# Other wait counts between projections, transposes and attention bursts in a two-layer hybrid decoder kernel

## The chip, the cores and the metric

The kernel runs on one core of a Trainium2 chip. The metric is the device time of one execution in microseconds (us); a kernel's time is the median of its runs. The five engines of a core work side by side, each on its own list of instructions, and meet through semaphores: PE (matmuls and transposes), DVE (vector), ACT (scalar, activation functions), POOL and SP (which here issues the large loads).

## The reference

Two layers, each a token mixer and an FFN, on 256 tokens of width 1024, in 32-bit floats. The attention in the mixer has two head groups of 8 heads each; with 256 tokens the block-sparse group (MoBA) is plain causal attention over one block, and the DSA group keeps, for each query, the 64 keys that a small indexer scores highest.

```python
def token_mixer(h, w_in, g_moba_out, g_dsa_out, w_out, cos, sin):
    proj = h @ w_in
    mq, mk, mv, dq, dk, dv, qi, ki, wi = jnp.split(proj, offs, axis=-1)
    ...
    o_moba = moba_attention(mq, mk, mv)
    o_dsa = dsa_attention(dq, dk, dv, qi, ki, wi)
    o = jnp.concatenate([rms_norm(o_moba, g_moba_out), rms_norm(o_dsa, g_dsa_out)], axis=-1)
    return o @ w_out
...
for l in range(DEPTH):
    mod = c_act @ w_ada[l] + b_ada[l]
    sh_m, sc_m, gt_m, sh_f, sc_f, gt_f = jnp.split(mod[:, None, :], N_MOD, axis=-1)
    h = rms_norm(x, g_pre_mix[l]) * (1.0 + sc_m) + sh_m
    y = token_mixer(h, w_in[l], g_moba_out[l], g_dsa_out[l], w_out[l], cos, sin)
    x = x + gt_m * rms_norm(y, g_post_mix[l])
    h = rms_norm(x, g_pre_ffn[l]) * (1.0 + sc_f) + sh_f
    y = conv_glu_ffn(h, w_up_act[l], w_up_lin[l], w_conv[l], b_conv[l], w_down[l])
    x = x + gt_f * rms_norm(y, g_post_ffn[l])
```

## The kernel before

**Precision by splits.** Every weight comes from DRAM as a raw tile of 128x1024 floats. ACT rounds it to a high half `wh` (L139), DVE subtracts to get the low half `wl` (L140), and a product is three matmuls: high by high, high by low, low by high. There are five buffers for `wh` and five for `wl`, and a projection of 512 columns takes four of each, so only one tile of the next projection can be split ahead.

**Projections.** A mixer projects mq, mk, mv, dq, dk, dv (512 columns each) for two halves t of the tokens. `project` issues, per t, 16 matmuls with `wh` (two between yields) and then 8 with `wl` (three between yields), all at L391. Layer 0's indexer, mq and mk are computed earlier, in the opening stage; its mv comes first in what follows. ACT then scales and evicts a result (L353, or L801 for the values), DVE rotates its first columns (L357, L362).

**What runs beside a projection.** Everything else is a chain of Python generators in `Background`. Each `yield` of the main work is one tick; a chain's `yield n` means that it goes on n ticks later. So a wait of 5 ticks puts a chain's next step some 10 matmuls further down the recorded program. The chains that matter here:

- "T" and "D": `heads_T` waits, then transposes a head group of q or k (4 transposes at L368, a copy at L369). In layer 0 all steps of T (indexer, mq, mk) stand in one chain behind one another; a chain that has not ended is run out by `drain`, with no matmuls of a projection between its steps.
- "att": first the indexer (a burst of matmuls at L411, relus L431 on ACT, weighted sums L434 on DVE), which waits until T is empty; then `attend` for each group. It works in three sets. A set is a burst of scores (L411) into PSUM banks 4 and 5, DVE's maxima (L475) and ACT's exponentials (L479), a scaling by the reciprocal of the sums (L482, then L485 on ACT or L487 on DVE), two `turn`s (4 transposes each, L494, and a copy L496) and, once the next set's scores are issued, a burst of `values` (L411) with its squares (L517, L518 on ACT; L520, L522 on DVE).
- "top0", "top1": `choose` finds the 64 best keys by eight pairs of MAX (L445) and MATCH_REPLACE (L446) on DVE.
- "out": `group_out` normalizes a head group (two short matmuls L549, a power on POOL, a transpose L556, then L560 to L562).
- "sf" and "gt": `gemv_v` on DVE (L189) and `gemv_p` on PE (a burst of 32 matmuls printed at L411, its transposes L210) compute the adaLN modulation from more weights.

**Order.** A scheduler places the recorded instructions on each engine's list; the order of recording is its main input. The loads are different: SP issues them from the stream in the order in which `load` was called, and the DRAM layout follows that order. A load waits until one of six `raw` buffers is free.

Of the kernel before, what the change touches and what calls it, by code (L numbers as in the profile page):

```python
# [17 lines left out]
D = 1024  # L18
# [56 lines left out]
def trunk(ctx: ExitStack, tc, plan, x, c, stream, small, rope, out):  # L75
# [8 lines left out]
    bg = Background()  # L84
# [7 lines left out]
    def tp_bank():  # L92
        tps["n"] += 1
        return bank(tps["free"][tps["n"] % len(tps["free"])])
# [4 lines left out]
    def big(name, dt=F32):  # L99
        return wrk.tile([128, 4, S], dt, name=name, tag="big", bufs=6)  # L100

    def tiny(n):
        return wrk.tile([128, n], F32, name=f"tiny{n}", tag=f"tiny{n}", bufs=8)


    st = {"off": 0, "behind": ()}
# [257 lines left out]
    def heads_T(src, dst, t, wait):  # L364
        yield wait
        p = tp_bank()
        for j in range(4):
            nc.tensor.transpose(p[:, 128 * j:128 * j + 128], src[:, 128 * j:128 * j + 128], ident)  # L368
        nc.scalar.copy(dst[:, :, 128 * t:128 * t + 128], p.rearrange("p (j t) -> p j t", j=4))  # L369
# [83 lines left out]
    def attend(qT, kT, v, masks, k0, oh, ol, ready):  # L453
# [36 lines left out]
        def turn(i, par):  # L490
            e = live[i, par][0]
            tp = tp_bank()
            for j in range(4):
                nc.tensor.transpose(tp[:, 128 * j:128 * j + 128], e[:, 128 * j:128 * j + 128], ident)  # L494
            eT = t2()
            nc.scalar.activation(out=eT, in_=tp, func=AF.Copy)  # L496
            live[i, par][0] = eT

        def values(i):

            t, b = sets[i]
            nb = t + 1
            nh = 4 // nb
            eT = [live.pop((i, par))[0] for par in range(2)]
            if t not in outs:
                outs[t] = [wrk.tile([128, 512], F32, name="o", tag="o", bufs=3), []]
            po = tp_bank()
            vk = [v[:, 2 * k:2 * k + 2, :].rearrange("p a b -> p (a b)") for k in range(nb)]
            head = lambda j, par: 64 * (2 * (b * nh + j) + par)
            burst([(po[64 * par:64 * par + 64, 128 * j:128 * j + 128],  # L510
                    vk[k][:, head(j, par):head(j, par) + 64],
                    eT[par][:, 128 * (j * nb + k):128 * (j * nb + k) + 128],
                    dict(start=k == 0, stop=k == nb - 1))
                   for j in range(nh) for k in range(nb) for par in (1, 0)])
            sq = t2()
            n = 128 * nh
            nc.scalar.activation(out=sq[:, :n], in_=po[:, :n], func=AF.Square)  # L517
            nc.scalar.activation(out=outs[t][0][:, n * b:n * b + n], in_=po[:, :n], func=AF.Copy)  # L518
            if nh == 4:
                nc.vector.tensor_tensor(out=sq[:, :256], in0=sq[:, :256], in1=sq[:, 256:], op=OP.add)  # L520
            ss = wrk.tile([128, 128], F32, name="ss", tag="ss", bufs=2)
            nc.vector.tensor_tensor(out=ss, in0=sq[:, :128], in1=sq[:, 128:256], op=OP.add)  # L522
            outs[t][1].append(ss)
# [3 lines left out]
        for i in range(len(sets)):  # L527
            while masks is not None and sets[i][0] not in masks:
                yield 1
            scores(i)  # L530
            if i:
                while sets[i - 1][0] not in ready:
                    yield 1
                values(i - 1)
                if sets[i - 1][0] != sets[i][0]:
                    bg.add("out", group_out(sets[i - 1][0], *outs[sets[i - 1][0]], k0, oh, ol))
            yield 3
            turn(i, 0)
            yield 1
            turn(i, 1)  # L540
            yield 2
# [3 lines left out]
    def group_out(t, o, ss, k0, hh, hl):  # L545

        p = tp_bank()
        for i, part in enumerate(ss):
            nc.tensor.matmul(p[:, :1], lhsT=part, rhs=mean, start=i == 0, stop=i == len(ss) - 1)  # L549
        s = tiny(1)  # L550
        nc.vector.tensor_scalar(out=s, in0=p[:, :1], scalar1=EPS, scalar2=None, op0=OP.add)
        r = tiny(1)
        nc.gpsimd.tensor_tensor(out=r, in0=s, in1=mhalf, op=OP.pow)
        yield 7
        p = tp_bank()[:, :128]
        nc.tensor.transpose(p, r.to_broadcast([128, 128]), ident)  # L556
        ks = slice(k0, k0 + 4)
        tt = slice(128 * t, 128 * t + 128)
        ov = o.rearrange("p (k t) -> p k t", k=4)
        nc.vector.tensor_tensor(out=ov, in0=ov, in1=p[:, None, :].to_broadcast([128, 4, 128]), op=OP.mult)  # L560
        nc.scalar.activation(out=hh[:, ks, tt], in_=ov, func=AF.Copy)
        nc.vector.tensor_tensor(out=hl[:, ks, tt], in0=ov, in1=hh[:, ks, tt].bitcast(F32), op=OP.subtract)  # L562
        st["out"] += 1
        yield
# [198 lines left out]
    for l in range(DEPTH):  # L763

        qiT = big("qT")
# [3 lines left out]
        def idx_out(b, t, a):  # L769
            if b == 0:  # L770
                qs[t] = t2()
                kis[t] = wrk.tile([128, 128], F32, name="ki", tag="ki", bufs=2)
                wis[t] = wrk.tile([128, 8], F32, name="wi", tag="wi", bufs=2)
            q, ki = qs[t], kis[t]
            rope_out(a[:, :256].rearrange("p (h d) -> p h d", d=HD),
                     q[:, 256 * b:256 * b + 256].rearrange("p (h d) -> p h d", d=HD), t, True, 4)
            if b == 0:
                rope_out(a[:, None, 256:320], ki[:, None, :64], t, False, 1)
                nc.scalar.activation(out=wis[t], in_=a[:, 320:], func=AF.Copy, scale=8.0 ** -0.5)
                nc.vector.tensor_copy(ki[:, 64:], ki[:, :64])  # L780
                return
            bg.add("T", heads_T(q, qiT, t, 5))
            bg.add("T", ki_T(ki, t))

        def ki_T(ki, t):
# [2 lines left out]
            nc.scalar.copy(kiT[:, 128 * t:128 * t + 128], p[:, :128])  # L788
            yield 1

        def qk_done(dst, is_q, chain="T", wait=5):
            def f(t, a):
                r = t2()
                rope_out(a.rearrange("p (h d) -> p h d", d=HD), r.rearrange("p (h d) -> p h d", d=HD), t, is_q, 8)
                bg.add(chain, heads_T(r, dst, t, wait))
            return f
# [8 lines left out]
        def run_project(name, done, first=()):  # L805
            late = "h" if name in ("ia", "ib") else "w" if name != "dv" else None
            bg.run(project(l, name, hh, hl, (0, 1, 2), done, first, late))
# [17 lines left out]
        masks = {}  # L825
# [20 lines left out]
        dqT, dkT, dv = big("qT"), big("kT"), big("v")  # L846
        if l == 0:
            bg.add("sf", gemv_v(l, 32, 40, 9))
        run_project("dq", qk_done(dqT, True, "D", 10))
        run_project("dk", qk_done(dkT, False, "D", 7))  # L850
        bg.add("att", attend(dqT, dkT, dv, masks, 4, oh, ol, ready[1]))
        run_project("dv", v_done(dv, ready[1]))
        bg.drain("T", "D", "ada", "gt")
# [210 lines left out]
```

## Time and profile before

| | |
|---|---|
| median of 3 runs | 690.02 us (689.62 to 690.02) |
| profiled execution | 689.88 us, of it 688.1 us span |
| granted TensorE clock | 0.999 of full speed |
| PE busy | 664.8 us, 97% |
| DVE busy | 547.6 us, 80% |
| ACT busy | 424.8 us, 62% |
| chain that ended last | PE 76%, DVE 12%, ACT 6%, issue 3% |

The span is the stretch from the first to the last instruction of the profiled execution; about 1.8 us lie around it. Busy shares are averages over stages with different limits. The chain that ended last is followed backwards from the last instruction, at each step to what released it. On a timeline a bracket such as [1.09 <-DVE tiny L475] says how long the engine was idle before the instruction, and what ended the wait.

### The profile page before, as it was taken

The numbers are of one execution on the slowest core, as the hardware profiler recorded it, in microseconds if no ns is written. First come the engines' busy times: TensorE is split into PE (matmuls) and PEld (weight loads), VectorE is DVE, ScalarE is ACT, GpSimd is POOL, SyncE is SP. The second block draws the span as 40 slices with busy tenths as digits, with TensorE's granted clock in tenths as the row PEclk, the third lists the DMA queues.
The fourth block names the chain that finished last, engine by engine and source line by source line (L and its number), as shares of the span: only waits on it lengthen the run. The fifth ranks groups of instructions, "written<-read, shape, count | busy, mean of one in ns | idle before, by whom it ended". The sixth has DMA issues, their size and how long they took to land.

```text
span 688.1 us, 11317 instructions
## 1 busy us (share of the span) xinstructions
PE 664.8 (97%) x4329; PEld 569.6 (83%) x4329; DVE 547.6 (80%) x1085; ACT 424.8 (62%) x787; POOL 26.2 (4%) x56
## 2 busy tenths in 40 slices
PE   7999898999999999999999999999999999999996
PEld 4887676777999999999988677777789999999994
DVE  5878999878899999897679985677689886666553
ACT  5556687886955555555576558878696555555441
POOL 1000000002000000000020000000200000000001
PEclk9999999999999999999999999999999999999999
DMA  8999558963499998987436642346246885655001
GB/s 362 419 415 372 181 203 332 370 219 123 183 332 379 379 361 340 340 328 281 168 140 245 275 133 114 123 168 220 103 172 232 320 316 183 217 184 184 1 1 61
DMA packets 24518, 163.04 MB, mean 237 GB/s; under 512 B 3312, under 2 KB 3728, under 8 KB 6160
## 3 DMA queue, kind: packets, MB, share of 16 engines
q1 hardware_dynamic: 23184, 159.77, 61.8%
q0 software_dynamic: 704, 2.11, 1.0%
q8 instruction: 34, 0.56, 0.3%
q10 hardware_dynamic: 576, 0.43, 0.2%
q14 instruction: 20, 0.16, 0.1%
HBM read 161.24 MB, written 1.06 MB: 236 GB/s over the span
## 4 chain that ended last, share of the span: by engine, by line
PE 76%; DVE 12%; ACT 6%; issue 3%; POOL 1%; DMA 1%; SPq 0%; POOLq 0%; DVEq 0%; ACTq 0%
PE b L569 18%; PE b L567 18%; PE b L568 18%; PE b L391 12%; PE b L726 3%; DVE wl L140 3%; PE b L411 2%; DVE iscore L434 2%; ACT t L479 1%; DVE iscore L446 1%; ACT t L254 1%; DVE tiny L445 1%; PE b L494 1%; DVE raw L684 1%; DMA raw<-in_stream_dram 1%
## 5 line engine op out<-in xcount | busy, mean ns | idle before, releaser
L140 DVE TENSOR_TENSOR wl<-raw,wh 128x1024 fp32r<-128x1024 f32 (+1 forms) x146 | 172.8, 1195 | 36.9 <-ACT wh L139 31.3
L567 PE MATMUL b<-hh,wh 128*128 128x256 f32 x640 | 179.9, 281 | 0.0
L569 PE MATMUL b<-hl,wh 128*128 128x256 f32 x640 | 179.6, 281 | 0.0
L568 PE MATMUL b<-hh,wl 128*128 128x256 f32 x640 | 179.6, 281 | 0.0
L139 ACT ACTIVATE wh<-raw 128x1024 fp32r<-128x1024 f32 (+1 forms) x146 | 149.0, 1047 | 41.9 <-PE b L569 37.0
L568 PEld LDWEIGHTS b<-hh,wl 128*128 128x128 f32 x640 | 122.5, 191 | 1.3
L567 PEld LDWEIGHTS b<-hh,wh 128*128 128x128 f32 x640 | 120.2, 188 | 1.5
L569 PEld LDWEIGHTS b<-hl,wh 128*128 128x128 f32 x640 | 120.1, 188 | 0.0
L189 DVE SCALAR_TENSOR_TENSOR raw<-raw,crow 128x1024 f32<-128x1024 f32 x72 | 86.6, 1218 | 1.9 <-DMA raw<-in_stream_dram 1.9
L391 PE MATMUL b<-wh,hh 128*128 128x512 f32 (+1 forms) x184 | 73.0, 399 | 0.1
L391 PE MATMUL b<-wh,hl 128*128 128x512 f32 (+1 forms) x184 | 68.5, 387 | 0.0
L140 DVE TENSOR_TENSOR dl<-raw,dh 128x1024 fp32r<-128x1024 f32 (+2 forms) x47 | 56.8, 1211 | 13.2 <-ACT dh L139 12.4
L139 ACT ACTIVATE dh<-raw 128x1024 fp32r<-128x1024 f32 (+2 forms) x47 | 49.6, 1060 | 25.6 <-PE b L568 25.6
L944 ACT ACTIVATE t<-b,smt 128x256 f32<-128x256 f32 x44 | 25.1, 571 | 57.9 <-PE b L569 57.9
L567 PE MATMUL b<-dh,t 128*128 128x512 f32 x152 | 59.7, 393 | 0.0
L568 PE MATMUL b<-dh,t 128*128 128x512 f32 x152 | 59.6, 392 | 0.0
L569 PE MATMUL b<-dl,t 128*128 128x512 f32 x152 | 59.2, 389 | 0.0
L391 PE MATMUL b<-wl,hh 128*128 128x512 f32 (+1 forms) x184 | 55.6, 392 | 1.0 <-DVE wl L140 1.0
L391 PEld LDWEIGHTS b<-wh,hh 128*128 128x128 f32 x184 | 34.7, 189 | 8.7 <-issue 1.7
L391 PEld LDWEIGHTS b<-wl,hh 128*128 128x128 f32 x184 | 33.8, 189 | 7.2 <-DVE wl L140 1.4
L391 PEld LDWEIGHTS b<-wh,hl 128*128 128x128 f32 x184 | 33.8, 188 | 6.2 <-issue 0.6
L945 DVE SCALAR_TENSOR_TENSOR t<-b,smt,t 128x255 f32<-128x255 f32 x44 | 21.1, 480 | 20.6 <-ACT t L944 20.4
(172 smaller groups left out, 1098.5 us busy)
## 6 DMA issues: line engine op xcount, KB each, us to landing
raw<-in_stream_dram SPq DMA_DIRECT2D x143, 1024.0 KB, 5.9
raw<-in_stream_dram SPq DMA_DIRECT2D x8, 804.0 KB, 9.6
gate<-gated POOLq DMA_DIRECT2D x4, 512.0 KB, 6.5
xt<-in_x_dram SPq DMA_DIRECT2D x2, 512.0 KB, 4.3
raw<-in_stream_dram SPq DMA_DIRECT2D x1, 984.0 KB, 5.1
out_dram<-xt SPq DMA_DIRECT2D x2, 256.0 KB, 2.1
raw<-in_stream_dram SPq DMA_DIRECT2D x1, 328.0 KB, 4.2
out_dram<-xt ACTq DMA_DIRECT2D x1, 256.0 KB, 2.1
```

The source lines that it names most:

```text
L139: put(nc.scalar.activation(out=hi[:, :n], in_=raw, func=AF.Copy))
L140: put(nc.vector.tensor_tensor(out=lo[:, :n], in0=raw, in1=hi[:, :n].bitcast(F32), op=OP.subtract))
L189: nc.vector.scalar_tensor_tensor(out=ri, in0=ri, scalar=1.0, in1=crow, op0=OP.mult, op1=OP.mult, accum_out=mods[l][:, j + i:j + i + 1])
L391: mm = lambda l_, k, i, start=False, stop=False: nc.tensor.matmul(a[:, :n], lhsT=l_[:, k, tt], rhs=w[k][i], start=start, stop=stop)
L411: ins = nc.tensor.matmul(out, lhsT=lhsT, rhs=rhs, **flags)
L434: nc.vector.scalar_tensor_tensor(out=sc, in0=r[:, j * nk:j * nk + nk], scalar=wi[:, h:h + 1], in1=fill[:, 256 - nk:] if first else sc, op0 ...
L567: nc.tensor.matmul(y, lhsT=hh, rhs=wh, start=first, stop=False)
L568: nc.tensor.matmul(y, lhsT=hl, rhs=wh, start=False, stop=False)
L569: nc.tensor.matmul(y, lhsT=hh, rhs=wl, start=False, stop=last)
L726: pin(nc.tensor.matmul(acc[n, t], lhsT=y[:, k, 128 * t:128 * t + 128], rhs=w[k, u][part][:, c:c + m],  start=k == 0 and y is hh and part = ...
L944: nc.scalar.activation(out=z, in_=p[:, :256], func=AF.Identity, scale=w2[:, i:i + 1], bias=bc[:, i:i + 1])
L945: nc.vector.scalar_tensor_tensor(out=z[:, 1:], in0=p[:, :255], scalar=w1[:, i:i + 1], in1=z[:, 1:], op0=OP.mult, op1=OP.add)
```

## The change

Five wait counts change. In `attend` the distance from a set's scores (and the values of the set before) to its first turn goes from 3 ticks to 6, except in the last set of the DSA group. In `group_out` the distance from the sum of squares to the transpose of its root goes from 7 to 10 for the first outputs. The waits ahead of `heads_T` go from 5 to 6 (indexer q), 5 to 8 (mq, mk), 10 to 12 (dq) and 7 to 9 (dk). No computation is added or removed.

```diff
@@ attend
-            yield 3
+            yield 3 if masks is not None and i == 2 else 6
             turn(i, 0)
@@ group_out
-        yield 7
+        yield 7 if st["out"] > 2 else 10
@@ idx_out
-            bg.add("T", heads_T(q, qiT, t, 5))
+            bg.add("T", heads_T(q, qiT, t, 6))
@@ qk_done
-        def qk_done(dst, is_q, chain="T", wait=5):
+        def qk_done(dst, is_q, chain="T", wait=8):
@@ the mixer
-        run_project("dq", qk_done(dqT, True, "D", 10))
-        run_project("dk", qk_done(dkT, False, "D", 7))
+        run_project("dq", qk_done(dqT, True, "D", 12))
+        run_project("dk", qk_done(dkT, False, "D", 9))
```

In layer 0 the chain T holds six `heads_T`: two of the indexer's q and four of mq and mk. Their waits and steps are some 32 ticks before and some 46 now, while mv's projection, the only one that runs beside them, gives 20. What is left is run out by `drain`, so more of it stands behind mv's last matmul with no projection between. The waits of "gt" and "sf" go on counting in that time: the first burst of `gemv_p` and one more pair of `gemv_v` tiles now come ahead of dq. The stream changes with it. Before, its order was (V for a `gemv_v` tile, p for one of `gemv_p`): V28, dq, dq, p16, p18, V30, V32, dk, dk. Now it is V28, p16, p18, V30, dq, dq, V32, p20, p22, V34, dk, dk. Layer 1's stream is the same.

ACT's list right behind mv's eviction in layer 0 (L801). Before, the first two of dq's splits (L139) stood ahead of all of the indexer's relus (L431), the other two behind the first pair:

```order
L801 ACTIVATE v<-b_696 128x512
L369 COPY qT<-b_741 128x4x128
L369 COPY kT<-b_750 128x4x128
L139 ACTIVATE wh<-raw 128x1024 x2
L369 COPY kT<-b_757 128x4x128
L431 ACTIVATE t_774<-b_764 128x512
L431 ACTIVATE t_780<-b_765 128x512
L139 ACTIVATE wh<-raw 128x1024 x2
L431 ACTIVATE t_827<-b_821 128x512
```

The same place of ACT's list now, from the first relu on:

```order
L431 ACTIVATE t_782<-b_772 128x512
L369 COPY kT<-b_758 128x4x128
L369 COPY kT<-b_765 128x4x128
L431 ACTIVATE t_788<-b_773 128x512
L431 ACTIVATE t_835<-b_829 128x512
L431 ACTIVATE t_839<-b_830 128x512
L206 ACTIVATE t_862<-b_845 128x512
L431 ACTIVATE t_877<-b_871 128x512
L139 ACTIVATE wh<-raw 128x1024 x2
L431 ACTIVATE t_881<-b_872 128x512
L139 ACTIVATE wh<-raw 128x1024 x2
```

dq's first split has moved behind five of the six relus. On PE the indexer's two wide bursts (into b_829 and b_830, then b_871 and b_872, the same two banks) now follow one another without a matmul between them, and dq's first matmul comes behind them.

DVE's list at the same place, as a difference. The L140 rows without a sign are dq's first two low halves; they stand in both:

```order
+L189 SCALAR_TENSOR_TENSOR raw,mod_99<-raw,crow 128x1024 x2
+L434 SCALAR_TENSOR_TENSOR iscore<-t_835,wi,fill 128x256
+L192 TENSOR_TENSOR mod_99<-mod_99,smt 128x8
+L445 MAX tiny_864<-iscore 128x8
+L434 SCALAR_TENSOR_TENSOR iscore<-t_835,wi,iscore 128x256
+L211 TENSOR_REDUCE mod_99<-b_891 128x4
+L434 SCALAR_TENSOR_TENSOR iscore<-t_839,wi,iscore 128x256
+L446 MATCH_REPLACE iscore<-tiny_864,iscore 128x128
+L434 SCALAR_TENSOR_TENSOR iscore<-t_839,wi,iscore 128x256
 L140 TENSOR_TENSOR wl<-raw,wh 128x1024 x2
-L434 SCALAR_TENSOR_TENSOR iscore<-t_774,wi,fill 128x128
-L434 SCALAR_TENSOR_TENSOR iscore<-t_774,wi,iscore 128x128 x3
```

Before, dq's low halves were the first thing behind the six `gemv_v` rows of V24 to V28. Now the eight narrow L434 and three pairs of MAX and MATCH_REPLACE (above this piece), V30's two L189 and four wide L434 come first; one MAX and two wide L434 stand between the second and the third low half.

ACT's list around dk's splits in layer 0, before. The exponentials L479 with t_966 and t_977 are set 1 of the MoBA group, L517 and L518 belong to set 0's values:

```order
L139 ACTIVATE wh<-raw 128x1024
L496 ACTIVATE t_949<-b_944 128x512
L139 ACTIVATE wh<-raw 128x1024 x2
L479 ACTIVATE t_966,tiny_969<-t_966,tiny_965 128x256 x2
L517 ACTIVATE t_997<-b_988 128x512
L485 ACTIVATE t_966<-t_966,rs 128x256 x2
L479 ACTIVATE t_977,tiny_980<-t_977,tiny_976 128x256 x2
L518 ACTIVATE o<-b_988 128x512
L485 ACTIVATE t_977<-t_977,rs 128x256 x2
L139 ACTIVATE wh<-raw 128x1024
```

The same work on ACT now, where t_1010 and t_1021 are set 1 and L353 evicts dq's second half:

```order
L479 ACTIVATE t_1010,tiny_1013<-t_1010,tiny_1009 128x256 x2
L479 ACTIVATE t_1021,tiny_1024<-t_1021,tiny_1020 128x256
L485 ACTIVATE t_1010<-t_1010,rs 128x256 x2
L479 ACTIVATE t_1021,tiny_1024<-t_1021,tiny_1020 128x256
L517 ACTIVATE t_1041<-b_1032 128x512
L518 ACTIVATE o<-b_1032 128x512
L485 ACTIVATE t_1021<-t_1021,rs 128x256 x2
L353 ACTIVATE t_1073<-b_959 128x512
L139 ACTIVATE wh<-raw 128x1024 x4
```

All four of dk's splits have moved behind set 1's work and the eviction. On PE, between dq's last matmul and dk's first, there now stand set 2's scores, dq's four transposes, an L549 and four of set 1's L494, and nothing else.

In layer 1 the four transposes of mk's first half move from behind 12 to behind 19 matmuls of the projection that follows, those of its second half likewise; mq's second half moves from behind three to behind six high-half matmuls. DVE's list there keeps the same rows ahead of mv's low halves, in nearly the same order.

## Rows read from the trace of the kernel before

**Rows 1.** The page: busy time of each engine, share of the span, instructions.

```profile
PE 664.8 (97%) x4329; PEld 569.6 (83%) x4329; DVE 547.6 (80%) x1085; ACT 424.8 (62%) x787; POOL 26.2 (4%) x56
```

**Rows 2.** Busy time of each engine in stretches; then clock, DMA share, GB/s.

```profile
53.00:163.00 110.00, 104.40 (x664) 77.75 (x663) 98.86 (x265) 80.79 (x179) 6.38 (x11) 1.00 0.71 264
70.00:90.00 20.00, 17.95 (x111) 12.64 (x110) 19.89 (x75) 13.95 (x32) 0.00 (x0) 1.00 0.50 177
357.00:490.00 133.00, 128.76 (x754) 101.06 (x753) 102.73 (x266) 93.42 (x200) 6.34 (x11) 1.00 0.47 175
200.00:220.00 20.00, 20.00 (x139) 18.52 (x138) 20.00 (x34) 10.83 (x17) 0.60 (x1) 1.00 0.97 369
```

**Rows 3.** Timeline of PE in layer 0's mixer: start, length, instruction, idle before.

```profile
71.01 1.13 PE L411 MATMUL b<-kiT,qT 64*128 64x256 f32 x8 [0.27 <-ACT t L431]
...
83.10 1.13 PE L411 MATMUL b<-kT,qT 64*128 64x256 f32 x8 [1.09 <-DVE tiny L475]
...
85.20 0.63 PE L494 MATMUL b<-ident,t 128*128 128x128 f32 x4 [0.54 <-DVE rs L482]
...
109.71 0.50 PE L391 MATMUL b<-wl,hh 128*128 128x512 f32 x1 [1.04 <-DVE wl L140]
...
116.31 0.32 PE L556 MATMUL b<-ident,tiny 128*128 128x128 f32 x1 [1.21 <-POOL tiny L553]
...
130.84 0.63 PE L494 MATMUL b<-ident,t 128*128 128x128 f32 x4 [0.51 <-DVE t L487]
```

**Rows 4.** Timeline of PE: mv's last pass, and a burst of gemv_p.

```profile
63.89 2.10 PE L391 MATMUL b<-wl,hh 128*128 128x512 f32 x8
...
94.47 1.93 PE L411 MATMUL b<-raw,cs 128*32 128x256 f32 x32
```

**Rows 5.** Timeline of ACT in layer 0's mixer.

```profile
67.47 2.03 ACT L139 ACTIVATE wh<-raw 128x1024 fp32r<-128x1024 f32 x2
...
72.70 1.12 ACT L431 ACTIVATE t<-b 128x512 f32<-128x512 f32 x2
...
90.47 0.50 ACT L479 ACTIVATE t<-t,tiny 128x256 f32<-128x256 f32 x1
...
94.26 0.91 ACT L485 ACTIVATE t<-t,rs 128x256 f32<-128x256 f32 x2
...
98.31 0.59 ACT L353 ACTIVATE t<-b 128x512 f32<-128x512 f32 x1
```

**Rows 6.** Timeline of DVE in layer 0's mixer.

```profile
68.58 2.36 DVE L140 TENSOR_TENSOR wl<-raw,wh 128x1024 fp32r<-128x1024 f32 x2 [2.79 <-ACT wh L139]
...
71.24 1.13 DVE L434 SCALAR_TENSOR_TENSOR iscore<-t,wi,iscore 128x128 f32<-128x128 f32 x3
...
80.34 1.22 DVE L189 SCALAR_TENSOR_TENSOR raw<-raw,crow 128x1024 f32<-128x1024 f32 x1
...
84.38 0.67 DVE L487 TENSOR_TENSOR t<-t,rs 128x512 f32<-128x512 f32 x1
...
87.16 0.61 DVE L445 MAX8 tiny<-iscore 128x8 f32<-128x128 f32 x2
...
89.51 0.41 DVE L475 CUSTOM_DVE_ANT_0 t<-b,lateneg 128x256 f32<-128x256 f32 x1
```

**Rows 7.** Timeline of SP's queue while mv is projected: six loads.

```profile
48.73 17.42 SPq L112 DMA_DIRECT2D raw<-in_stream_dram  x6
```

**Rows 8.** Timeline of PE in layer 1's mixer.

```profile
395.35 0.63 PE L368 MATMUL b<-ident,t 128*128 128x128 f32 x4 [1.15 <-ACT wh L139]
...
402.12 0.63 PE L368 MATMUL b<-ident,t 128*128 128x128 f32 x4 [0.65 <-DVE t L362]
...
403.52 1.99 PE L391 MATMUL b<-wl,hh 128*128 128x512 f32 x8
...
424.54 0.35 PE L549 MATMUL b<-mean,ss 128*128 128x1 f32 x2 [0.22 <-DVE ss L522]
...
458.10 0.63 PE L494 MATMUL b<-ident,t 128*128 128x128 f32 x4 [0.43 <-DVE t L487]
```

**Rows 9.** Timeline of DVE ahead of mv's last pass in layer 1.

```profile
401.89 2.35 DVE L140 TENSOR_TENSOR wl<-raw,wh 128x1024 fp32r<-128x1024 f32 x2
```

## The prediction

> **What bounds the kernel now.** I read the page first: PE is busy 97% of the span, DVE 80%, ACT 62% [rows 1]. So the end is set by PE's list, and only its idle time can be won. The stretches [rows 2] say where that is. In the FFN (200 to 220 us as a sample) PE is busy 20.00 of 20.00, and this change touches nothing there. In layer 0's mixer (53 to 163) it is busy 104.40 of 110, in layer 1's (357 to 490) 128.76 of 133: 5.6 and 4.2 us idle. The reader should look at DVE in the same rows: between 70 and 90 us it is busy 19.89 of 20. There PE waits for a full DVE list, and a wait taken away at one place comes back at the next unless DVE also has less to do ahead of it. The granted clock is 1.00 in all of these rows (the higher level), so all durations below are at one clock. Third, PE's timeline gives the single waits of layer 0: 0.27, 1.09, 0.54, 1.04, 1.21 and 0.51, sum 4.7 us, most of the 5.6 [rows 3]; of layer 1: 1.15, 0.65, 0.22 and 0.43 [rows 8].
>
> **Prices.** A projection's matmul goes every 0.23 us ((1.99 - 0.39) / 7, eight in a row [rows 8], the last one being 0.39 long). A narrow or a wide indexer burst or a burst of scores is 1.1 [rows 3], a `gemv_p` burst 1.9 [rows 4], four transposes some 0.35 to 0.4. On DVE an L140 or an L189 takes 1.2, a narrow L434 0.38, an L487 0.67, an L475 of 256 columns 0.4, a MAX 0.3 [rows 6]; a MATCH_REPLACE I put at the same 0.3 to 0.4, as an estimate. On ACT an L139 takes 1.0, a relu 0.56, an L479 of 256 columns 0.50, an L485 0.46, an L353 0.59 [rows 5]. The work is the same before and after. So the sum is made of PE's waits alone, the new ones less the old ones. I went along the new lists of PE, DVE and ACT from mv's last pass (63.89 us, 2.10 long [rows 4]) on, and let each instruction start when its own list and its inputs allow.
>
> **Layer 0, mv to dq.** First, the second wide indexer burst writes the two banks that the first one's relus must have left. Before, some 8 matmuls of dq stood between the two, and the wait of this kind was 0.27 at most [rows 3]; now nothing does, and two relus are 1.12 [rows 5]: **1.1 us**, 0.8 at least. Second, dq's first matmul needs dq's first split, which stands behind a relu of that second burst: 0.56 + 1.0, less 0.4 for the transposes of `gemv_p` that PE has meanwhile: **1.1**, 0.6 at least. Third, dq's low halves. DVE gets its first relu at about 68 us. Up to the third L140 it then has 8 narrow L434 (3.0), 3 pairs of MAX and MATCH_REPLACE that depend on each other (2.1), V30's two L189 (2.4), four wide L434 and four small operations (2.7), two L140 (2.4), two wide L434 and a MAX (1.1) and the L140 itself (1.2): 14.9, to 82.9. PE's first dq matmul stands at 74.9 by the waits above; 17 matmuls, set 0's scores and four more bring it to the third low half at 80.8. That is a wait of 2.0, and 0.6 more for the fourth. Being the end of two long chains, it may also be 0: I take **1.0**. dq's loads stand three loads later in the stream. Before, they were the first two of a row of six, of which the last was issued by 66.15 (48.73 + 17.42 [rows 7]); now they are the fourth and fifth of it. The first split wants them at about 73.9, more than 7 us after that. So they cost nothing; if one were late, ACT's L139 and all behind it would be.
>
> **Set 0 of MoBA.** Its turns wait for L487 at the end of DVE's list, as set 1's scores and the turns did before (1.09 and 0.54). I find 1.5 against 1.6: **0**.
>
> **dq to dk.** Set 2's scores need banks 4 and 5, so set 1's four L475. When set 1's scores end, DVE has two L487 (1.3), some 0.8 of small operations, twelve MAX and MATCH_REPLACE (3.6) and the four L475 (1.5): 7.2. PE has the two waits above (1.5), two turns (0.9), eight low-half matmuls (1.9) and set 0's values (1.1): 5.4. Wait 1.8, I take **1.5**, 0.5 at least. Then dk's first matmul: ACT must do four L479 (2.0), four L485 (1.8), L517 and L518 (some 1.2), L353 (0.6) and the first L139 (1.0), 6.6 in all, of which some 0.7 before the last L475 ends. PE has set 2's scores, four transposes, an L549 and one turn, 2.0 in all. That makes 3.9, seen at the L549 or at dk's first matmul. Before, three of dk's four splits stood ahead of the exponentials, and PE had no wait there. I take **2.4**; 1.0 if set 1's work runs more tightly.
>
> **Rest of layer 0.** dk's splits and set 2's exponentials now share one stretch of ACT; set 2's turns and values wait 0 to 2.8, I take **0.6**. The DSA group waits 0.4 (0 to 1.1). Three L189 more lie ahead of dk's low halves than before; later DVE has that much less, and I credit the three waits from 109 us on (1.04, 1.21, 0.51) and the first 0.27 in full: **-3.0**, or -1.5 if two stay in another form.
>
> Layer 0: 1.1 + 1.1 + 1.0 + 1.5 + 2.4 + 0.6 + 0.4 - 3.0 = **+5.1**. Bounds: 0.8 + 0.6 + 0 + 0.5 + 1.0 + 0 + 0 - 3.0 = -0.1, and 1.1 + 1.1 + 2.6 + 1.8 + 3.9 + 2.8 + 1.1 - 1.5 = 12.9.
>
> A rule stands behind this way of reckoning. The trace shows strict order for PE: at 395.35 four transposes held it for 1.15 us [rows 8] while the projection's next matmuls stood behind them. For DVE and ACT no row here decides it. The Trainium skill (PSUM — Partial Sum Buffer, Engine vs sequencer instructions) says that the queues of these engines are strict first in, first out, and it speaks against this change: a V tile that comes in early delays the low halves behind it. Without such order, dq's third term would fall to 0 and dk's to 1.0, 2.4 less.
>
> **Layer 1.** Here the longer wait does what a longer wait can do: mk's transposes move from behind 12 to behind 19 matmuls, 1.6 us later, and their waits of 1.15 and 0.65 [rows 8] go. But mv's last pass needs its fourth low half. Its third and fourth L140 end at 404.24 (401.89 + 2.35 [rows 9]); the seventh matmul of that pass starts at 403.52 + 6 x 0.23 = 404.9 [rows 8]. DVE goes without a gap up to there, and keeps the same rows ahead. So PE can come only 0.65 earlier, and the other 1.15 turn into a wait for L140: **-0.65**, or -1.8 if DVE gets there earlier. The later L549 and turn save 0.22 and 0.43, and longer runs of set work may cost 0 to 1.0, taken 0.4: **-0.25**. Layer 1: **-0.9**, between -2.5 and +0.4.
>
> **Sum.** +5.1 - 0.9 = +4.2 on the profiled execution's 689.88 (688.1 of span and 1.8 around it; the median of the runs shown, 690.02, is 0.1 above): 694.1. Walking along lists by hand adds up waits that the chip may partly merge, so I round down to **693.6**.
>
> **Rivals.** (a) *The sums by list are too gloomy, and layer 1 pays:* DVE's total is unchanged, so in the full stretches PE's waits only take each other's place. Then layer 0 is at its lower bound, -0.1, and layer 1 at -2.5: 687.3. For it speaks that DVE idles 2.79 us before dq's first low half now [rows 6], which earlier work could fill; against it that ACT's list puts dk's splits behind L353 by order, whatever DVE does. It decides if PE stands less than 1 us ahead of dk. (b) *A draw:* layer 0 between +0.5 and +2 for low costs at dk, layer 1 near -1: 690. (c) *ACT becomes the bound from dk on:* set 2's turns, the values and the dv splits all queue behind dk's four L139; 0.6 becomes 2.8 and dk's wait 3.9: layer 0 +8.8, 697.8. For it speaks ACT's new order; against it that ACT is busy only 80.8 of 110 there [rows 2]. (d) *DVE and ACT let ready work pass waiting work:* then the two terms named above fall by 2.4: 691.7.
>
> **Chances.** My forecast, 691.5 to 696: 0.46. (a) with anything below 688.6: 0.22. (b) with the stretch up to 691.5: 0.19, of which 0.13 lies within 0.2% (1.4 us, about what a measurement of this kernel can tell from no change). (c): 0.13. (d) lies inside the forecast's and (b)'s share. So faster 0.22, same 0.13, slower 0.65. The range reaches to 687.6, into (a), and to 698.5, which takes in most of (c).
>
> **What would show it.** In the changed kernel's profile: a second wide indexer burst that waits about 1 us for L431; dq's first matmul waiting for ACT's L139; set 2's scores waiting for L475, then an L549 or dk's first matmul waiting 1 us or more; no wait at 109 or 116 us. In layer 1: no wait at mk's transposes, but a low-half matmul of mv waiting for L140. I am wrong if dk's first matmul comes without a wait, or if layer 1's mixer is 2 us shorter.

## The result and the profile after

The changed kernel takes 697.44 us (median of 4 runs, 696.9 to 698.19) against 689.89 of the kernel before (4 runs, 689.62 to 690.02): ratio 1.0106, 95% interval 1.0093 to 1.0118, so 7.5 us slower. The forecast was 693.6 with a range of 687.6 to 698.5. The side was right and the time lies in the range, but 3.8 us of the loss were not in the sum. The profiled execution took 697.8, of it 696.0 span. The four runs lie in two pairs with different mean granted clocks: 696.9 and 697.08 at 0.996 and 0.997, 697.8 and 698.19 at 0.992 and 0.993.

The page after, busy time of each engine and further down the granted clock in 40 slices:

```profile
PE 667.5 (96%) x4329; PEld 572.7 (82%) x4329; DVE 550.6 (79%) x1085; ACT 425.4 (61%) x787; POOL 25.8 (4%) x56
...
PEclk9999989999999999999999999999999999999998
```

PE is busy 2.7 us longer than in [rows 1] with as many instructions: some of them ran longer. The clock's 8 in the sixth slice says where to look. The stretches, with PE, PEld, DVE, ACT, POOL busy, clock, DMA share and GB/s; the first row is layer 0's mixer in the kernel before, the others are the changed kernel:

```profile
53.00:162.58 109.58, 103.98 (x660) 77.33 (x658) 98.44 (x264) 80.50 (x178) 6.34 (x10) 1.00 0.71 264
53.00:169.42 116.42, 106.81 (x659) 80.19 (x658) 100.88 (x264) 80.42 (x176) 6.77 (x10) 0.97 0.69 253
...
70.00:90.00 20.00, 15.97 (x99) 11.01 (x90) 19.70 (x63) 11.51 (x27) 0.00 (x0) 1.00 0.78 276
90.00:110.00 20.00, 16.75 (x110) 11.63 (x110) 19.64 (x67) 13.80 (x29) 1.45 (x1) 0.83 0.48 172
110.00:130.00 20.00, 20.00 (x124) 16.43 (x120) 15.26 (x33) 14.58 (x29) 2.14 (x3) 1.00 0.97 369
```

The first two rows end where layer 0's mixer ends. PE's idle time in it grows from 5.60 to 9.61 us, by 4.0, and its busy time from 103.98 to 106.81, by 2.8, for the same work. Between 70 and 90 us PE has lost 2.0 us against [rows 2], while DVE is as full as before. The first transposes of the boundary behind the mixers (PE's timeline, L274) mark the ends of the stages. They stand at 162.58 us before and 169.42 after in layer 0: 6.84 later. The boundary behind layer 0's FFN moves by 6.95 (351.53 to 358.48), so the FFN changes by 0.1, and that behind layer 1's mixer by 7.87 (492.27 to 500.14): layer 1's mixer is 0.92 longer, where -0.9 was forecast, so its sign was wrong.

PE's timeline of layer 0's mixer after, the rows that wait (start, length, instruction, idle before and what ended it), and at 100.62 dk's first matmul, which does not:

```profile
68.56 1.93 PE L411 MATMUL b<-raw,cs 128*32 128x256 f32 x32 [0.24 <-ACT kT L369]
...
72.77 1.14 PE L411 MATMUL b<-kiT,qT 64*128 64x256 f32 x8 [1.21 <-ACT t L431]
...
75.57 0.50 PE L391 MATMUL b<-wh,hh 128*128 128x512 f32 x1 [1.08 <-ACT wh L139]
...
82.30 0.73 PE L391 MATMUL b<-wl,hh 128*128 128x512 f32 x2 [0.33 <-DVE wl L140]
83.43 0.74 PE L391 MATMUL b<-wl,hh 128*128 128x512 f32 x2 [0.41 <-DVE wl L140]
...
89.68 0.63 PE L494 MATMUL b<-ident,t 128*128 128x128 f32 x4 [1.01 <-DVE t L487]
...
90.94 0.52 PE L494 MATMUL b<-ident,t 128*128 128x128 f32 x3 [0.17 <-ACT t L496]
...
95.50 1.13 PE L411 MATMUL b<-kT,qT 64*128 64x256 f32 x8 [1.32 <-DVE tiny L475]
98.39 0.90 PE L368 MATMUL b<-ident,t 128*128 128x128 f32 x3 [1.76 <-ACT o L518]
...
100.62 0.80 PE L391 MATMUL b<-wh,hh 128*128 128x512 f32 x1
...
138.14 0.63 PE L494 MATMUL b<-ident,t 128*128 128x128 f32 x4 [0.19 <-DVE t L487]
...
146.35 0.35 PE L549 MATMUL b<-mean,ss 128*128 128x1 f32 x2 [0.24 <-DVE ss L522]
...
154.57 0.44 PE L494 MATMUL b<-ident,t 128*128 128x128 f32 x2 [0.34 <-ACT t L485]
...
163.25 0.74 PE L567 MATMUL b<-wh,hh 128*128 128x512 f32 x2 [1.04 <-ACT hh L561]
164.27 0.50 PE L568 MATMUL b<-wh,hl 128*128 128x512 f32 x1 [0.29 <-DVE hl L562]
```

They sum to 9.63 us, against 4.66 in [rows 3]; there two more waits belong to the list, 0.29 at 152.66 (L556) and 0.43 at the boundary (162.58), so the waits grow by 4.25. From 72 to 96 us they are the waits of the forecast, at its instructions; the next, 1.76, stands one step earlier than forecast. The waits of 1.04 and 1.21 that stood at 109 and 116 us are gone. Two things are new: the last two rows, in the output projection, and what follows the wait of 1.76. ACT's timeline there:

```profile
95.99 0.89 ACT L485 ACTIVATE t<-t,rs 128x256 f32<-128x256 f32 x2
96.79 0.49 ACT L479 ACTIVATE t<-t,tiny 128x256 f32<-128x256 f32 x1
...
97.28 0.57 ACT L517 ACTIVATE t<-b 128x512 f32<-128x512 f32 x1
97.76 0.57 ACT L518 ACTIVATE o<-b 128x512 f32<-128x512 f32 x1
98.24 0.90 ACT L485 ACTIVATE t<-t,rs 128x256 f32<-128x256 f32 x2
99.04 0.58 ACT L353 ACTIVATE t<-b 128x512 f32<-128x512 f32 x1
99.52 1.99 ACT L139 ACTIVATE wh<-raw 128x1024 fp32r<-128x1024 f32 x2
```

This is the row of work that the forecast set ahead of dk's first split. PE meets it one step earlier: dq's transposes (L368) want the PSUM bank that set 0's values hold until L518 has read them. The stretches of 2 us around this place:

```profile
94.00:96.00 2.00, 0.68 (x5) 0.48 (x6) 2.00 (x12) 1.50 (x7) 0.00 (x0) 1.00 0.00 0
96.00:98.00 2.00, 0.63 (x6) 0.20 (x4) 2.00 (x9) 2.00 (x7) 0.00 (x0) 1.00 0.00 0
98.00:100.00 2.00, 1.61 (x7) 1.38 (x8) 1.64 (x7) 2.00 (x5) 0.21 (x1) 0.56 0.00 0
100.00:102.00 2.00, 2.00 (x7) 1.63 (x7) 2.00 (x6) 2.00 (x3) 1.24 (x1) 0.50 0.15 25
102.00:104.00 2.00, 2.00 (x6) 1.54 (x5) 2.00 (x4) 2.00 (x4) 0.00 (x0) 0.50 0.83 283
104.00:106.00 2.00, 2.00 (x8) 1.52 (x7) 2.00 (x3) 0.46 (x2) 0.00 (x0) 0.74 0.98 320
```

In the first two PE is busy 0.68 and 0.63 of 2 us; then the granted clock falls to 0.50, which is 1.2 GHz, and is back by 106. PE looks full from 100 us on and does 6 or 7 matmuls in 2 us. In the kernel before, the clock of the same mixer was 1.00 [rows 2].

PE's timeline of layer 1's mixer after:

```profile
409.67 0.73 PE L391 MATMUL b<-wl,hh 128*128 128x512 f32 x2 [0.46 <-DVE wl L140]
410.80 0.73 PE L391 MATMUL b<-wl,hh 128*128 128x512 f32 x2 [0.40 <-DVE wl L140]
...
476.64 0.35 PE L549 MATMUL b<-mean,ss 128*128 128x1 f32 x2 [0.43 <-DVE ss L522]
484.11 0.73 PE L567 MATMUL b<-wh,hh 128*128 128x512 f32 x2 [0.85 <-ACT hh L561]
485.46 0.44 PE L494 MATMUL b<-ident,t 128*128 128x128 f32 x2 [0.18 <-ACT t L485]
494.25 0.74 PE L567 MATMUL b<-wh,hh 128*128 128x512 f32 x2 [1.03 <-ACT hh L561]
```

mk's waits of 1.15 and 0.65 [rows 8] are gone, and mv's low halves wait 0.86 in their place, as forecast in kind. But the output projection now waits too: 0.85 and 1.03 for L561, where it did not before.

Three questions follow. Do the losses of the two layers stand apart? Does the fall of the clock explain the part of layer 0 that no wait shows? And which edit makes the waits for L561?

### The profile page after: what moved, and what is told of

Read it like the earlier page. It is cut to its first block, busy times and chain, and to the rows that moved or that the text cites. A ratio compares the mean times of both kernels' runs of the same rounds, so it can differ in the third digit from the quotient of the medians.

```text
span 696.0 us, 11313 instructions
## 1 busy us (share of the span) xinstructions
PE 667.5 (96%) x4329; PEld 572.7 (82%) x4329; DVE 550.6 (79%) x1085; ACT 425.4 (61%) x787; POOL 25.8 (4%) x56
## 4 chain that ended last, share of the span: by engine, by line
PE 73%; DVE 14%; ACT 8%; issue 3%; DMA 1%; POOL 1%; SPq 0%; POOLq 0%; DVEq 0%; ACTq 0%
PE b L568 18%; PE b L569 17%; PE b L567 17%; PE b L391 12%; DVE wl L140 3%; PE b L726 3%; PE b L411 2%; DVE raw L189 2%; ACT t L479 2%; DVE iscore L434 2%; ACT wh L135 1%; PE b L494 1%; DVE iscore L446 1%; DVE wl L136 1%; DVE raw L684 1%
## 5 line engine op out<-in xcount | busy, mean ns | idle before, releaser
L140 DVE TENSOR_TENSOR wl<-raw,wh 128x1024 fp32r<-128x1024 f32 (+1 forms) x146 | 172.8, 1197 | 32.5 <-ACT wh L139 29.9
L139 ACT ACTIVATE wh<-raw 128x1024 fp32r<-128x1024 f32 (+1 forms) x146 | 148.7, 1045 | 43.9 <-PE b L569 36.1
L189 DVE SCALAR_TENSOR_TENSOR raw<-raw,crow 128x1024 f32<-128x1024 f32 x72 | 86.8, 1222 | 0.9 <-DMA raw<-in_stream_dram 0.9
L140 DVE TENSOR_TENSOR dl<-raw,dh 128x1024 fp32r<-128x1024 f32 (+2 forms) x47 | 56.9, 1212 | 14.6 <-ACT dh L139 11.7
L139 ACT ACTIVATE dh<-raw 128x1024 fp32r<-128x1024 f32 (+2 forms) x47 | 49.6, 1058 | 25.6 <-PE b L568 25.6
L391 PE MATMUL b<-wl,hh 128*128 128x512 f32 (+1 forms) x184 | 57.1, 394 | 1.6 <-DVE wl L140 1.6
```

What stands on the lines that cost most here:

```text
L139: put(nc.scalar.activation(out=hi[:, :n], in_=raw, func=AF.Copy))
L140: put(nc.vector.tensor_tensor(out=lo[:, :n], in0=raw, in1=hi[:, :n].bitcast(F32), op=OP.subtract))
L189: nc.vector.scalar_tensor_tensor(out=ri, in0=ri, scalar=1.0, in1=crow, op0=OP.mult, op1=OP.mult, accum_out=mods[l][:, j + i:j + i + 1])
L391: mm = lambda l_, k, i, start=False, stop=False: nc.tensor.matmul(a[:, :n], lhsT=l_[:, k, tt], rhs=w[k][i], start=start, stop=stop)
```

## Experiments

All ratios are against runs of the kernel before on the same chip (its medians there 689.83 to 690.22), with their 95% intervals. Edits are shown against the changed kernel or the one before, as named.

**The change in one layer alone** (`l_now["l"]` is the layer; the other edits are cut in the same way; shown against the changed kernel). Layer 0:

```diff
-            bg.add("T", heads_T(q, qiT, t, 6))
+            bg.add("T", heads_T(q, qiT, t, 6 if l == 0 else 5))
...
-        def qk_done(dst, is_q, chain="T", wait=8):
+        def qk_done(dst, is_q, chain="T", wait=8 if l == 0 else 5):
```

> The longer waits in layer 0 alone; layer 1 has the old ones. By the stage ends of the two profiles (first boundary at 162.58 before, 169.42 now; second 6.95 us later; third 7.87 later) layer 0 costs 6.9 us and layer 1 another 0.9: 696.8. By the term of the prediction, in which layer 1 gains 0.9, it would be above the full change: 698.3.

Measured: 696.58, ratio 1.0093 (1.0078 to 1.0109). Layer 1, with `l == 1`:

> The longer waits in layer 1 alone. By the stage ends 690.8 (0.9 above before). By the prediction's term for layer 1 (-0.9): 689.0. If the two layers' costs are tied to each other, neither.

Measured: 690.71, ratio 1.0013 (1.0004 to 1.0022). 6.7 and 0.85 us against the same kernel before make the whole 7.5: the layers add, layer 0 carries nine tenths, and layer 1 loses by itself.

**The T chain's waits put back in the changed kernel:**

```diff
-            bg.add("T", heads_T(q, qiT, t, 6))
+            bg.add("T", heads_T(q, qiT, t, 5))
...
-        def qk_done(dst, is_q, chain="T", wait=8):
+        def qk_done(dst, is_q, chain="T", wait=5):
```

> The changed kernel with the waits ahead of the indexer's and the MoBA group's transposes put back (6 to 5, 8 to 5); attend, group_out, dq and dk keep the longer waits. Theory: layer 0's loss comes from the steps of the chain T that are run out behind mv, with the loads and the gemv burst that this pulls ahead of dq; then most of 7.5 us goes, 691 to 692. Rival: the longer distances inside attention and at dq and dk cost it; then 695 or more.

Measured: 693.99 (five runs, 692.64 to 694.32; the profiled one took 692.64), ratio 1.0053 (1.004 to 1.0065). Neither guess hit. In the profile layer 0's mixer ends at 163.47, only 0.9 later than before: there the T waits make up 6.0 of the 6.84. Layer 1's mixer is 142.54 long (140.74 before, 141.66 in the changed kernel): there the T waits gain 0.9 and the other edits cost 1.8. The output projection waits for L561 here too, and then 0.29 for L562:

```profile
157.28 0.73 PE L567 MATMUL b<-wh,hh 128*128 128x512 f32 x2 [1.27 <-ACT hh L561]
```

**Spare matmuls for the clock**, into a bank that nothing uses there; their results are not read:

```diff
+            fill_in = l_now["l"] == 0 and masks is None and i == 2
+            spare = [(bank(3), negi, lateb[:, None, :].to_broadcast([128, 4, 128]), dict(start=True, stop=True))]
...
-                   for j in range(nh) for par in (1, 0)])
+                   for j in range(nh) for par in (1, 0)] + (spare * 8 if fill_in else []))
```

and 6 more behind set 0's values in the same way.

> The changed kernel with 14 spare matmuls (results unused, into a free bank) where PE stands idle in layer 0 at 94 to 98 us: six behind set 0's values, eight behind set 2's scores. Theory: the clock, which fell to 0.50 of full speed behind that idle stretch and stayed there for 7 us, holds, and dk's matmuls go every 0.23 instead of 0.43 us: 1.8 us less, 695.6. Rival: PE would only wait longer for dk's splits on ACT: no change, 697.4. If the spare matmuls get in the way: more than 697.4.

Measured: 696.09, ratio 1.0091 (1.0078 to 1.0105): 1.35 faster than the changed kernel by the medians (they are from two chips; the kernel before is the same on both within 0.03). The two intervals overlap, the runs do not: 695.72 to 696.84 here, 696.9 to 698.19 there. The clock did not fall:

```profile
96.00:98.00 2.00, 2.00 (x14) 1.02 (x13) 2.00 (x7) 2.00 (x8) 0.00 (x0) 1.00 0.00 0
98.00:100.00 2.00, 1.55 (x10) 0.74 (x7) 2.00 (x9) 2.00 (x6) 0.00 (x0) 1.00 0.00 0
100.00:102.00 2.00, 1.31 (x8) 1.10 (x9) 2.00 (x7) 2.00 (x3) 0.54 (x1) 1.00 0.41 61
102.00:104.00 2.00, 2.00 (x12) 1.61 (x11) 2.00 (x4) 2.00 (x3) 0.00 (x0) 1.00 0.82 319
```

12 matmuls go between 102 and 104 where 6 went, and layer 0's mixer ends at 167.83, 1.6 earlier. More work made the kernel faster. So keeping the clock up is worth 1.4 to 1.6 of layer 0's 6.84. That is less than the 2.8 us by which PE's busy time grew: at the full clock PE meets other waits here, 0.34 at 99.03 and 0.80 at 100.69, in place of the 1.76. The edit is not the clock alone either: the scheduler also spread set 1's four transposes among dk's matmuls.

**The T waits alone, in one layer of the kernel before.** Layer 0, then layer 1 (with `l == 1`):

```diff
-            bg.add("T", heads_T(q, qiT, t, 5))
+            bg.add("T", heads_T(q, qiT, t, 6 if l == 0 else 5))
...
-        def qk_done(dst, is_q, chain="T", wait=5):
+        def qk_done(dst, is_q, chain="T", wait=8 if l == 0 else 5):
```

> The kernel before with one edit: the longer waits of the T chain in layer 0 alone. Theory: these waits by themselves move set work against dq and dk and cost what their removal gave back from the changed kernel, 5.9 us, with the fall of the granted clock near dk in it: 695.8 us. Rival: the cost needs the longer D and set waits beside them: alone they cost under 2 us, 692 or less.

Measured: 694.19, ratio 1.0057 (1.0044 to 1.0069): +4.1, between the two guesses. The same first waits stand there (PE 72.81, 75.61, 82.35, 83.48), a turn waits 2.56 for L518 at 98.06, and the clock falls as well (0.50 between 100 and 102). The longer D, set and output waits come on top of it.

> The kernel before with one edit: the longer waits of the T chain (6 for the indexer's heads, 8 for mk's and mq's) in layer 1 alone. Theory: this is the part that pays; mk's two transpose waits vanish, mv's fourth low half takes a part of them back: layer 1's mixer 0.9 us shorter, layer 0 unchanged, 689.0 us. Rival: layer 1 gives it back before its output projection, 689.9 us, no change.

Measured: 688.88, ratio 0.998 (0.9972 to 0.9989): 1.2 faster. Layer 1's mixer is 139.78 long, 0.96 less, and waits at mv's low halves (402.86 and 404.00) for 0.44 and 0.40, as above.

**The output sets' wait put back to 7 in the changed kernel:**

```diff
-        yield 7 if st["out"] > 2 else 10
+        yield 7
```

> The changed kernel with the wait of 10 before the output sets' transpose put back to 7. Theory: the waits for L561 and L562 in the output projection of both layers (1.2 + 0.46 in layer 0, 1.0 + 1.2 in layer 1) come from this 10, since the transpose then stands too close ahead of the matmuls that read its result; they vanish: 693.8 us, or up to 695 if part of them comes back at the boundary's transposes. Rival: they come from the sets' work being late by the other edits, so they stay: 697.4 us.

Measured: 703.03, ratio 1.0191 (1.0177 to 1.0205). Both guesses fell: it is 5.6 slower than the changed kernel. PE's timeline and then ACT's at the place:

```profile
161.92 0.32 PE L556 MATMUL b<-ident,tiny 128*128 128x128 f32 x1 [0.30 <-POOL tiny L553]
164.57 0.73 PE L567 MATMUL b<-wh,hh 128*128 128x512 f32 x2 [2.33 <-ACT hh L561]
```

```profile
161.42 1.06 ACT L139 ACTIVATE wh<-raw 128x1024 fp32r<-128x1024 f32 x1 [0.67 <-PE b L568]
162.50 1.28 ACT L595 ACT_TABLE_LOAD   x1
163.79 0.20 ACT L595 ACTIVATE tiny<-mhalf 128x1 f32<-128x1 f32 x1
163.90 0.61 ACT L561 ACTIVATE hh<-o 128x512 fp32r<-128x512 f32 x1
```

The wait of 7 lets the scheduler place a load of an activation table (1.28) and a split ahead of L561, where the changed kernel has the table load earlier (159.97). Behind the idle 2.33 the clock is 0.50 between 166 and 168. The larger part of the loss lies in layer 1, whose mixer is 144.84 long against 141.66 in the changed kernel. There PE waits 0.94 at the last L556, 1.57 for L561 and 0.39 for L562 (495.11 to 498.61), and the clock falls too:

```profile
498.00:500.00 2.00, 1.61 (x4) 1.16 (x4) 1.22 (x2) 1.44 (x4) 0.00 (x0) 0.50 0.80 233
```

The Trainium skill (ScalarE: Activation LUTs, What ACT_TABLE_LOAD costs) gives such a load some 1.28 us and adds a drain of 1.38. The trace agrees on the first; ACT's instruction ahead of the load ends 0.02 us before it and the next one starts 0.01 us after its end, so no such drain shows in these rows.

**Layer 1's T waits, the sets' 6 and the D chain's 12 and 9 without the rest** (against the changed kernel, with the edit above):

```diff
-            bg.add("T", heads_T(q, qiT, t, 6))
+            bg.add("T", heads_T(q, qiT, t, 6 if l == 1 else 5))
...
-        def qk_done(dst, is_q, chain="T", wait=8):
+        def qk_done(dst, is_q, chain="T", wait=8 if l == 1 else 5):
```

> The changed kernel with the T chain's waits put back in layer 0 alone and the output sets' wait put back to 7 in both layers; left of the change are layer 1's T waits, the sets' 6 and the D chain's 12 and 9. Theory: layer 0 is then 1 us shorter than before (0.9 longer with 2.0 of waits for L561 and L562 in it), layer 1 1.3 us shorter (0.9 longer with 2.2 of such waits): 687.6 us, below both kernels. Rival: the waits in the output projection only stand in place of waits at the boundary, and the result is 689 to 690 us.

Measured: 698.82, ratio 1.0125 (1.0111 to 1.0139). Again the wrong side, with waits of 2.22 and 0.82 for L561 and L562 at 159.12 and 160.68. As in the kernel above, a split and the table load (157.06) stand ahead of L561, and the clock falls behind it in both layers (0.54 between 160 and 162, 0.50 between 492 and 498).

**The sets' distance back to 3 in the changed kernel, 6 alone in the kernel before, and the D waits alone:**

```diff
-            yield 3 if masks is not None and i == 2 else 6
+            yield 3
```

> The changed kernel with the distance from a set's scores to its first turn put back from 6 to 3 in all sets. Theory: the five longer distances push the last DSA set so late that only 2 matmuls are left between the last output transpose (L556) and the first one that needs its result; with 3 the list has 15 there in layer 0 and 19 in layer 1, so the waits for L561 and L562 (1.33 and 2.2 us) vanish: 693.9 us. Rival: that room is taken from elsewhere, or the cost lies in the D chain's 12 and 9 or in the T chain: 697 us.

Measured: 700.72, ratio 1.0159 (1.0145 to 1.0172): the theory fell. In spite of the 15 matmuls, layer 0's output projection is held at other instructions:

```profile
154.48 0.29 PE L556 MATMUL b<-ident,tiny 128*128 128x128 f32 x1 [0.91 <-ACT t L496]
...
157.90 0.50 PE L568 MATMUL b<-wh,hl 128*128 128x512 f32 x1 [0.74 <-DVE hl L562]
...
160.85 0.32 PE L556 MATMUL b<-ident,tiny 128*128 128x128 f32 x1 [0.85 <-POOL tiny L553]
```

These are 2.5 us, for 1.67 at the last turn and at L561 and L562 in the changed kernel. Now the first group's output (157.90) is the late one, and the transposes L556 themselves wait. Layer 1's mixer is 143.30 long, 1.64 more than in the changed kernel. So inside the change the longer distance saves time.

> The kernel before with one edit: the distance of 6 for 3 from a set's scores to its first turn. Theory: the room behind the last L556 goes from 13 and 16 matmuls to 6, 1.4 us, where the chain L560, L561, L562 wants some 2.2: waits of about 0.8 in each layer, 691.6 us. Rival: the longer distance takes waits at the turns away that are worth as much, 690 us or less.

Measured: 688.96, ratio 0.9988 (0.9979 to 0.9997). The rival was nearer: 0.9 faster, with no wait for L561; layer 1's mixer is 139.74 long, 1.0 less.

> The kernel before with one edit: the D chain's waits of 12 for 10 (dq) and 9 for 7 (dk). Theory: room behind the last L556 of 3 matmuls in layer 0 and 7 in layer 1, so waits of 1.3 and 0.6 and little else: 692 us. Rival: dq's and dk's transposes wait less in exchange, or the two ticks are lost in slack: 690 us.

Measured: 690.88, ratio 1.0019 (1.0009 to 1.0028): 1.05 slower, with one wait of the kind expected in layer 0, none in layer 1:

```profile
156.21 0.73 PE L567 MATMUL b<-wh,hh 128*128 128x512 f32 x2 [0.80 <-ACT hh L561]
...
463.96 0.63 PE L494 MATMUL b<-ident,t 128*128 128x128 f32 x4 [0.91 <-DVE t L487]
```

But this wait is not where the loss lies. In the profile layer 0's mixer ends at 162.83, only 0.25 later than before, since other waits there are shorter; layer 1's is 141.65 long, 0.91 more. A part of that is the turn at 463.96, which waits 0.91 for L487 where a turn waited 0.43 [rows 8]; the rest is not placed.

**The two edits that paid, together:**

```diff
-            yield 3
+            yield 3 if masks is not None and i == 2 else 6
...
-            bg.add("T", heads_T(q, qiT, t, 5))
+            bg.add("T", heads_T(q, qiT, t, 6 if l == 1 else 5))
...
-        def qk_done(dst, is_q, chain="T", wait=5):
+        def qk_done(dst, is_q, chain="T", wait=8 if l == 1 else 5):
```

> The kernel before with two edits: the longer T waits in layer 1 alone, and the distance of 6 for 3 from scores to turns in both layers. Theory: both edits paid in layer 1 (1.2 and 0.9 us) at different places, mk's transposes and the sets, and the last L556 keeps 9 matmuls of room in both layers, with which no wait was seen: 688.0 us. Rival: they take the same slack of the lists, so that the second one adds nothing: 688.9 us; or they disturb each other as in the changed kernel: over 690.

Measured: 688.14, ratio 0.9968 (0.9956 to 0.998), 2.1 faster than the kernel before on that chip (690.22). In the profile layer 1's mixer is 138.85 long, 1.9 less: the gains add. Layer 1's stretch:

```profile
363.00:491.00 128.00, 125.98 (x732) 99.57 (x730) 100.92 (x260) 90.01 (x193) 5.18 (x10) 1.00 0.49 180
```

PE is idle for 2.0 of 128 us, against 4.2 of 133 in [rows 2].

**What makes the waits for L561.** Between the last L556 and the first matmul that needs its result, PE's list holds some matmuls of other rows. Their number, counted in the lists (for the sets' 6 alone it is 8, not the 6 of the expectation), beside layer 0's idle time for L561 and L562 in the profile:

| kernel | matmuls between | idle |
|---|---|---|
| before | 13 | 0 |
| sets' 6 alone | 8 | 0 |
| D waits alone | 3 | 0.80 |
| changed | 2 | 1.04 + 0.29 |
| T waits put back | 1 | 1.27 + 0.29 |
| output wait put back | 0 | 2.33 |
| layer 1's T waits, sets' 6 and D waits | 0 | 2.22 + 0.82 |

The chain L560, L561, L562 behind a transpose takes some 1.5 us up to the first result (161.74, where L556 ends, to 163.25 in the changed kernel), the time of six or seven matmuls at 0.23, and the idle time falls as the number grows: from 1 to 3 each further matmul takes 0.23 or 0.24 off the wait for L561, its own time. The two rows with 0 have more than this gives, because ACT is late as well: with the outputs' wait put back, L560 ends at 162.97 and L561 starts at 163.90, behind the table load. Layer 1 fits the pattern: 2 matmuls and 1.03 in the changed kernel, 7 and none with the D waits alone. The wait of 0.85 at 484.11 there is of another kind: 8 matmuls stand ahead of it, and L561 is late (483.44) because ACT does four L479, L517 and L518 first. The sets run later in the program, so more of the output rows that could stand there have already gone ahead of them. That this number decides the wait at this place is a pattern over seven kernels, not an edit of that number alone. The number does not decide the total: with 15 between (sets' distance back to 3) the kernel was 10.9 slower than before.

## Why the prediction was right, and where its sum fell short

**Right, step by step.** The second wide indexer burst: 1.1 forecast, 1.21 measured. dq's first matmul: 1.1 and 1.08. The third and fourth low half: 1.0 and 0.74. Set 0's turns: 1.5 and 1.18, against 1.63 before. Set 2's scores: 1.5 and 1.32. The credit: 1.04, 1.21 and 0.27 gone in full, the 0.51 down to 0.19. dq's loads, three loads later, cost nothing: its first matmul waits for ACT's split, and that was priced. PE was driven by DVE's and ACT's lists in the order in which they stand (ACT's rows from 95.99 to 99.52 are its list, row by row), so rival (d) is out. In layer 1, mk's two waits turned into a smaller one at mv's low halves; alone this was worth 0.96, where 0.65 of it was forecast.

**Right in kind, off in place and size.** The wait ahead of dk, 2.4 with 0.6 for set 2: ACT's row of L479, L485, L517, L518, L353 and L139 was as listed, but it is set 0's bank, free only behind L518, that holds up dq's transposes, for 1.76. dk's first matmul then starts at 100.62, when the first split is done, and has no wait of its own. By its letter that is one of the prediction's signs of being wrong; the wait that it named stood one step earlier.

**Missed.** First, the granted clock: the sum said that all durations were at one clock, since every row of before showed 1.00. Behind the waits at 94 to 98 us, which the sum had forecast in kind, it fell: PE's busy time grew by 2.8, of which the spare matmuls won back 1.4 to 1.6. The sum's own waits, side by side, should have raised that question. The Trainium skill (TensorE: Matmul & The Clock Gate, Part 1: The HAM clock gate) states that an idle PE is gated down from 2.4 to 1.2 GHz; the rows above agree on the two levels, though PE was not idle throughout here, but busy 0.68 and 0.63 of 2 us.

Second, the output projection. The working ended with set 2 and the DSA group's 0.4; it did not follow the longer distances to the output transposes L556, behind which there was room before. That cost 1.33 in layer 0 and 1.88 in layer 1 (0.85 and 1.03). With the L549 there (0.43) this outweighs layer 1's gain: +0.92 for -0.9. The failed step is "longer runs of set work may cost 0 to 1.0, taken 0.4": in layer 1 the waits for L561 alone were 1.88. The bound of +0.4 for layer 1 did not come out of its terms either; with 1.0 for the set work they give -0.65 - 0.65 + 1.0 = -0.3.

Layer 0 in all: 4.0 more of idle time and 2.8 more of busy time make the 6.84. The busy time is where the low clock shows. So the waits came to less than the +5.1 of the sum, though 1.33 of them were not foreseen. The profiled execution lies 4.2 us above the forecast: 2.8 by PE's busy time, 1.8 by layer 1, 0.5 by the rounding and 0.1 by the FFN, less 1.1 by which layer 0's waits had been set too high.

**Rivals.** (c) gives 697.8, next to what was measured, but not by its mechanism: ACT does not bound PE from dk on, for PE is busy 20.00 of 20 between 110 and 130. Its number fits by accident. This touches the hit as well: 697.44 lies outside the 691.5 to 696 that the chances gave to the forecast itself, in the part of the range that was added for (c). So the side was earned by the mechanism, and the time lies in the range partly by luck. (b) fell with layer 0, which lost far more than 2. (a) fell for layer 0; in layer 1 a gain near its size can be had, 1.9, but by two of the edits alone.

**Open.** The edits do not add. Measured alone, they give +4.1 (T, layer 0), -1.2 (T, layer 1), -0.9 (sets) and +1.05 (D), +3.05 in all; together with the outputs' 10, which was not run alone, they give 7.5. By layers, in the profiles: in layer 1 the three edits alone give -0.96, -1.0 and +0.91, -1.05 in all, against +0.92; the difference of 1.97 is about the size of the waits for L561 there, 1.88, which none of the three kernels has. In layer 0 they give +4.16, -0.07 and +0.25 (boundaries at 166.74, 162.51 and 162.83), against 6.84. Of the 2.5 between, 0.53 are waits for L561 and L562 (1.33, less the 0.80 that the D waits have alone). The clock is below 1.00 from 98 to 106 us in the changed kernel and only from 98 to 104 with the T waits alone, but how much of the rest that is, is not shown. Why the sets' 3 costs 3.3 inside the change, while 3 costs only 0.9 in the kernel before, is not settled.

## What to carry to other kernels

A wait count in a program that a scheduler orders moves everything behind it, so follow a longer distance to the end of its chain: what is late last stands before the point where all chains must be done, and there nothing is left to cover it. Test each such count alone and by layer; here one change held edits worth -1.2, -0.9, +1.05 and +4.1, and the version with only the first two is 2.1 us faster than the kernel it started from. When a sum contains several waits of PE side by side, look whether the granted clock will hold through them.

## What was not expected of the hardware

The granted clock fell to 0.50 (1.2 GHz) after two stretches in which PE was busy 0.68 and 0.63 of 2 us, and 14 matmuls whose results nobody reads, put into these gaps, made the kernel 1.35 us faster. In the two kernels with the longest waits for L561, 2.22 and 2.33 us, it fell behind those waits too, in both layers. A load of an activation table, 1.28 us on ACT, held nothing up at 159.97 us in one kernel and helped to hold PE for 2.33 us in another, by its place in the list alone.
